# Setting aside rows for DMA engine 4 and raising the cap when levelling the last zero rows of an argmax-scatter kernel

## The chip, the cores and the metric

One core of one Trainium2 chip. The metric is device time in microseconds; lower is better. A run's time is the span of its profile plus about 1.75 us.

## The reference

```python
scores (8, 2048, 2048) float32, values (8, 2048, 2560) float32   # one fixed draw
best_j = argmax(scores, axis=2)
gathered = values[b, best_j]
out = zeros_like(values);  np.add.at(out, (b, best_j), gathered)
```

Row j of a batch of the output is values[b, j] times the number of score rows that chose j. In this draw 6131 output rows are zero (746 in the last batch), 5875 are copied once, and 4378 are scaled by a count of two or more. A row is 10,240 bytes.

## The kernel before: the parts that matter

The kernel moves everything by DMA: score tiles into a ring in SBUF; single rows straight from values to output; scaled rows by a gather, a multiply on ScalarE and a scatter; zero rows by scattering a tile of zeros. An indirect transfer has 128 slots, and slots whose index is out of bounds move nothing. Each of the 16 DMA engines serves eight of the 128 slots of a transfer, so where an index stands decides which engine does the row.

For the last batch's zeros the kernel chooses that. It adds up each engine's rows, adds FETCH (rows set aside for instruction fetches and other things that cost the engine time), and hands the last zero rows to the engines with the least work, at most CORR rows of correction for one engine:

```python
    ZLAST = 12
    FETCH = {2: 5, 3: 12}
    CORR = 56
    # [...]
    for e, n in FETCH.items():
        nc.vector.memset(fetch[:, e:e + 1], float(n))
    # [...] in level_engines: work = zero rows + 2 x scaled rows + fetch + copied rows, per engine
    top = max(work);  more = top - work                # condensed
    more = min(more, CORR) * (zeros <= 16 * (128 - CORR))
    even = ceil(max(zeros - sum(more), 0) / 16)
    quota = more + even                                # running sum; the last engine gets what is left
```

The lines after the second [...] are condensed; in the program each is one VectorE instruction on a 128x16 tile. The last engine (15) takes whatever remains after the running sum, so it gets less than its quota.

At the end GpSimd issues, for the last batch, five gathers, plain copies and zero transfers in turn, five scatters, and the last eight zero transfers with the last three plain copies between them; then it waits until all completions have been counted. Nothing is computed after the last transfer.

## Time and profile before

| | kernel before |
|---|---|
| median of the first 3 runs | 822.98 us (822.6 to 824.76) |
| DMA traffic | 347 MB, 16 engines over 90% busy in 39 of 40 slices |
| the profiled execution, taken apart from these runs | 825.77 us (span 824.0 us) |
| VectorE, the busiest compute engine | 73% |
| last transfer issued | 809.08 us after the start |
| last packet, last completion, end of the span | 821.6, 822.7, 824.0 us |

The lines are in the prediction. The view by windows is to be read as follows: the DMA share is the mean over 16 engines, so 0.0625 in a window of 1 us is one engine busy throughout; the sum of the shares after the first engine runs dry, laid end to end, is where perfectly level engines would stop.

### The profile page before, as it was taken

Reading aid. Unit: us, or ns where it says so; the run is one execution under the profiler, and the core shown is the slowest. Engines: PE = TensorE matmul, PEld = TensorE weight load, DVE = VectorE, ACT = ScalarE, POOL = GpSimd, SP = SyncE. Lnnn points to the kernel's source line nnn. Section 1 sums busy time; section 2 is a strip of 40 time slices with the busy share of each in tenths; the row PEclk is TensorE's granted clock in tenths of the full one; section 3 lists DMA queues with packets and bytes.
Section 4 is the critical chain, followed back from the end, with each engine's and each line's share of the span. In section 5 each row is a group of like instructions: output and inputs, shape, how many; then the busy total and the mean of one; then the engine's idle time right before and its main releaser. Section 6 shows DMA issues by size and latency. Waiting matters only on the chain.

```text
span 824.0 us, 2978 instructions
## 1 busy us (share of the span) xinstructions
PE 31.8 (4%) x786; PEld 29.1 (4%) x786; DVE 600.3 (73%) x737; ACT 168.1 (20%) x107; POOL 271.3 (33%) x277
## 2 busy tenths in 40 slices
PE   0211210000000000000000000000000000000000
PEld 0111110000000000000000000000000000000000
DVE  5887779999999999999999999999998000000000
ACT  6664730041012100023000032000320230230140
POOL 0027241011233504201513200615166356346442
DMA  9999999999999999999999999999999999999997
GB/s 385 426 437 429 433 412 410 441 419 425 427 423 427 428 427 435 429 428 420 429 427 421 429 428 430 433 428 412 426 425 424 423 427 422 424 424 422 425 425 288
DMA packets 44949, 347.12 MB, mean 421 GB/s; under 512 B 18662, under 2 KB 18662, under 8 KB 18662
## 3 DMA queue, kind: packets, MB, share of 16 engines
q0 software_dynamic: 38736, 212.67, 62.1%
q1 hardware_dynamic: 6192, 134.22, 38.0%
q8 instruction: 6, 0.10, 0.0%
q14 instruction: 15, 0.12, 0.0%
HBM read 354.42 MB, written 300.15 MB: 794 GB/s over the span
## 4 chain that ended last, share of the span: by engine, by line
DMA 35%; DVE 27%; another core or an unknown queue 23%; ACT 5%; POOL 5%; issue 4%; PE 0%; SPq 0%; ACTq 0%; POOLq 0%; DVEq 0%
DMA room<-in_values_dram,many_i 23%; DVE am L201 9%; DVE mx L200 9%; DMA out_dram<-room,many_i 8%; DVE mx L224 5%; ACT room L417 4%; DMA room<-in_scores_dram 4%; POOL out_dram L33 3%; ACT less L227 2%; POOL out_dram L182 2%; POOL room L177 1%; DVE oh L378 1%; DVE oh_lo L210 1%; DVE sole L234 0%
## 5 line engine op out<-in xcount | busy, mean ns | idle before, releaser
L201 DVE FIND_INDEX8 am<-mx,room 128x8 uint32<-128x2048 f32 x96 | 219.3, 2285 | 0.0
L200 DVE MAX8 mx<-room 128x8 f32<-128x2048 f32 x96 | 218.7, 2278 | 0.0
L417 ACT ACTIVATE room<-room,many_c 128x2560 f32<-128x2560 f32 x40 | 96.6, 2426 | 587.6 <-DMA room<-in_values_dram,many_i 587.6
L33 POOL DMA_INDIRECT out_dram<-in_values_dram,ones_i x128 | 130.3, 1018 | 106.3 <-DVE m L349 67.9
L182 POOL DMA_INDIRECT out_dram<-room,many_i x40 | 38.7, 966 | 258.0 <-ACT room L417 254.9
L177 POOL DMA_INDIRECT room<-in_values_dram,many_i x40 | 41.2, 1029 | 155.2 <-DMA out_dram<-room,many_i 137.0
L224 DVE MAX8 mx<-room 128x8 f32<-128x2048 f32 x32 | 72.8, 2286 | 11.4 <-DMA room<-in_scores_dram 11.4
L227 ACT ACTIVATE less<-room,mx 128x2048 bf16<-128x2048 f32 x32 | 64.0, 2001 | 38.4 <-DVE sole L234 17.4
L182 POOL DMA_INDIRECT out_dram<-zrow,zero_i x61 | 60.1, 985 | 18.6 <-issue 18.3
L218 PE MATMUL cnt_ps<-oh_hi,oh_lo 128*128 128x16 bf16 x96 | 6.1, 174 | 418.0 <-DVE oh_hi L214 418.0
L218 PEld LDWEIGHTS <-oh_lo 128*128 128x128 bf16 x96 | 6.3, 104 | 417.9 <-DVE oh_lo L210 397.9
L237 PEld LDWEIGHTS <-less 128*128 128x128 bf16 x512 | 16.1, 104 | 83.3 <-ACT less L227 59.6
L378 DVE TENSOR_TENSOR oh<-lo,fill_f 128x2048 f16<-128x2048 uint32 x8 | 18.3, 2291 | 0.3
L237 PE MATMUL cnt_ps<-sole,less 128*128 128x1 bf16 x512 | 18.1, 165 | 0.0
L210 DVE TENSOR_TENSOR oh_lo<-lo,lane_f 128x512 bf16<-128x512 uint32 x24 | 16.6, 693 | 0.4
L234 DVE TENSOR_SCALAR sole<-n_less 128x1 bf16<-128x1 f32 x32 | 4.8, 149 | 14.9 <-ACT less L227 14.7
L201 DVE MATCH_VALUE_LOAD am<-mx,room 128x8 f32 x96 | 8.8, 92 | 3.3
L235 PE MATMUL cnt_ps<-sole,minus 128*128 128x16 bf16 x32 | 5.5, 172 | 82.9 <-DVE sole L234 81.1
L396 PE MATMUL l_ps<-put,oh 128*128 128x32 f16 x128 | 4.7, 188 | 70.9 <-DVE put L393 70.9
L396 PEld LDWEIGHTS <-oh 128*128 128x128 f16 x128 | 4.6, 104 | 72.0 <-DVE oh L378 61.6
L227 ACT ACTIVATION_READ_ACCUMULATOR less<-room,mx 128x1 f32 x32 | 6.0, 186 | 0.0
L206 DVE TENSOR_SCALAR lo<-am 128x4 uint32<-128x4 uint32 x24 | 5.3, 222 | 0.8
(104 smaller groups left out, 80.7 us busy)
## 6 DMA issues: line engine op xcount, KB each, us to landing
room<-in_scores_dram SPq DMA_DIRECT2D x24, 4096.0 KB, 17.5
room<-in_scores_dram SPq DMA_DIRECT2D x9, 2048.0 KB, 13.1
room<-in_scores_dram SPq DMA_DIRECT2D x8, 1024.0 KB, 5.8
room<-in_scores_dram SPq DMA_DIRECT2D x2, 3072.0 KB, 13.9
out_dram<-in_values_dram,ones_i POOLq DMA_INDIRECT x128
out_dram<-zrow,zero_i POOLq DMA_INDIRECT x61
room<-in_values_dram,many_i POOLq DMA_INDIRECT x40, 45.0
out_dram<-room,many_i POOLq DMA_INDIRECT x40, 46.5
```

The source lines that it names most:

```text
L33: return eng.add_instruction(ins)
L177: note(nc.gpsimd.indirect_dma_start(out=v, out_offset=None, in_=values_flat[:, :], in_offset=bass.IndirectOffsetOnAxis(ap=idx, axis=0), bo ...
L182: note(nc.gpsimd.indirect_dma_start(out=out_flat[:, :], out_offset=bass.IndirectOffsetOnAxis(ap=idx, axis=0), in_=v, in_offset=None, bound ...
L200: nc.vector.max(out=mx[:], in_=rows)
L201: nc.vector.max_index(out=am[:, g, :], in_max=mx[:], in_values=rows)
L210: nc.vector.tensor_tensor(out=oh_lo[:], in0=lo[:].unsqueeze(2).to_broadcast([P, G, P]), in1=lane_f[:].unsqueeze(1).to_broadcast([P, G, P]) ...
L218: nc.tensor.matmul(out=cnt_ps[:], lhsT=oh_lo[:, k, :], rhs=oh_hi[:, k, :], start=(t == G - 1 and k == 0), stop=(t == NT - 1 and k == G - 1))
L224: nc.vector.max(out=mx[:], in_=rows)
L227: nc.scalar.activation(out=less[:], in_=rows, func=mybir.ActivationFunctionType.Sign, bias=mx[:, 0:1], scale=-1.0, accum_out=n_less[:])
L237: nc.tensor.matmul(out=cnt_ps[:, c:c + 1], lhsT=less[:, c * P:(c + 1) * P], rhs=w, start=False, stop=(t == NT - 1 and c == NT - 1))
L378: nc.vector.tensor_tensor(out=oh[:], in0=lo[:].unsqueeze(2).to_broadcast([P, NT, P]), in1=fill_f[:].unsqueeze(1).to_broadcast([P, NT, P]), ...
L417: nc.scalar.activation(out=v, in_=v, func=mybir.ActivationFunctionType.Copy, bias=0.0, scale=mc[:, k:k + 1])
```

## The change

Its intent: engine 4 was seen to end late, so 8 rows are set aside for it as well; engine 2 gets one fewer; and the cap that kept engines 9 and 12 from being filled is raised.

```diff
-    FETCH = {2: 5, 3: 12}
-    CORR = 56
+    FETCH = {2: 4, 3: 12, 4: 8}
+    CORR = 64
```

## The prediction

> **What bounds the kernel now.** I read the page first: its head, the table of slices and the queues.
>
> ```profile
> span 824.0 us, 2978 instructions
> PE 31.8 (4%) x786; PEld 29.1 (4%) x786; DVE 600.3 (73%) x737; ACT 168.1 (20%) x107; POOL 271.3 (33%) x277
> DMA  9999999999999999999999999999999999999997
> GB/s 385 426 437 429 433 412 410 441 419 425 427 423 427 428 427 435 429 428 420 429 427 421 429 428 430 433 428 412 426 425 424 423 427 422 424 424 422 425 425 288
> q0 software_dynamic: 38736, 212.67, 62.1%
> q1 hardware_dynamic: 6192, 134.22, 38.0%
> q8 instruction: 6, 0.10, 0.0%
> q14 instruction: 15, 0.12, 0.0%
> ```
>
> No compute engine is over 73% busy, while the 16 DMA engines are over 90% busy in 39 of 40 slices; queues 0 and 1 together hold 100% of their time. The kernel is bound by how long the DMA engines take over 20,762 rows of values and 134 MB of scores. Only the last slice is not full. The view by windows of the end, one window per microsecond (columns: width, five engines' busy time, granted clock, DMA share, GB/s), and the timeline's last line show what is left:
>
> ```profile
> 814.00:815.00 1.00, 0.00 (x0) 0.00 (x0) 0.00 (x0) 0.00 (x0) 0.00 (x0) 1.00 1.01 390
> 815.00:816.00 1.00, 0.00 (x0) 0.00 (x0) 0.00 (x0) 0.00 (x0) 0.00 (x0) 1.00 0.87 349
> 816.00:817.00 1.00, 0.00 (x0) 0.00 (x0) 0.00 (x0) 0.00 (x0) 0.00 (x0) 1.00 0.89 339
> 817.00:818.00 1.00, 0.00 (x0) 0.00 (x0) 0.00 (x0) 0.00 (x0) 0.00 (x0) 1.00 0.63 216
> 818.00:819.00 1.00, 0.00 (x0) 0.00 (x0) 0.00 (x0) 0.00 (x0) 0.00 (x0) 1.00 0.31 73
> 819.00:820.00 1.00, 0.00 (x0) 0.00 (x0) 0.00 (x0) 0.00 (x0) 0.00 (x0) 1.00 0.11 31
> 820.00:821.00 1.00, 0.00 (x0) 0.00 (x0) 0.00 (x0) 0.00 (x0) 0.00 (x0) 1.00 0.08 31
> 821.00:822.00 1.00, 0.00 (x0) 0.00 (x0) 0.00 (x0) 0.00 (x0) 0.00 (x0) 1.00 0.03 0
> 809.08 0.96 POOL L182 DMA_INDIRECT out_dram<-zrow,zero_i  x1 [0.30 <-issue]
> ```
>
> GpSimd issued its last transfer at 809.08, so what comes after is queued work draining, and the engines run dry at different times. The shares from 814 on add up to 1.01+0.87+0.89+0.63+0.31+0.11+0.08+0.03 = 3.93 us of all engines: perfectly level they would end at 817.9. The last packet ended at 821.6, so **3.7 us, 0.45%, is all that any levelling can win**. From 819 to 821, 31 GB/s is about one engine (425/16 = 27): one straggler.
>
> **Which engine.** The packet records of the trace carry time, queue and size but no engine. I chained them: on one engine a packet starts 4 ns before the last one ends, a row of 10,240 B takes 385 ns and a row skipped by the bounds check a 9 ns packet, so a row costs 381 ns and a skipped one 6. Which of an engine's eight rows of each transfer are real follows from the reference's own draw (6131 rows of zeros, 746 in the last batch; 5875 copied once; 4378 scaled), which gives every engine its own pattern; 15 of the 16 chains match one engine's pattern back over most of the run, the other (engine 9) back to 740 us. Ends of the chains, in us: engine 4 821.6; 10 819.8; 3 818.9; 11 818.9; 6 818.6; 14 818.6; 2 818.3; 5 818.1; 1 818.0; 8, 9 and 13 817.4; 7 and 0 816.6; 12 814.7; 15 814.5. The straggler is engine 4, by 1.8 us.
>
> **What the Trainium skill says.** "DMA: Bandwidth & Descriptors", section "The descriptor swizzle", gives partition to engine as 8*(p>>6)+((p>>2)&7); the index layout of this kernel is built on it, and the zero rows match the chains only so: the trace agrees. "Queues, rings and completion order" calls row 14 runtime-internal, one ring per engine; here the 15 packets of queue 14 fall in chains of engine 3 (about 8) and engine 2 (about 6), which is what FETCH answers to. "Latency and other measured facts" says engines 7 and 15 are usually slower; this trace disagrees: 15 ended first, 7 among the first four. "Anatomy of one DMA" says that a completion waits for the write's receipt: here the last data packet ended at 821.35 and the last six completions on the counter that the kernel waits for came at 821.78 to 822.73, 189 ns apart, so a tail of 0.43 us for one mark and 0.19 for each further one.
>
> **The change part by part.** Nothing is added to the stream but one more fill of a 128x1 column: the same row fills 59 ns at 1.1 us, and VectorE waits for its first scores until 5.5, so it costs nothing. The instructions of all other engines are the same. What changes is data: the quota of the last batch's 746 zero rows. I redid the kernel's arithmetic on the reference's draw. Load ahead of the last zeros, engines 0 to 15, before: 1275 1278 1269 1291 1264 1243 1244 1253 1240 1222 1269 1235 1217 1253 1236 1244; after, engine 2 has 1268 and engine 4 has 1272. The top (engine 3, 1291) stays. Corrections of engines 9 and 12 would be 69 and 74; the cap cut both to 56 and now cuts to 64. The even share stays 10. Real zero rows that move: engine 4 37 to 29 (-8), engine 2 32 to 33, engine 9 66 to 74 (+8), engine 12 66 to 74 (+8), engine 15, which takes what is left, 51 to 42 (-9). All others keep theirs.
>
> A moved row is worth 381-6 = 375 ns. If every engine otherwise runs as in this trace, the chains end at: engine 4 821.6-3.0 = 818.6; engine 9 817.4+3.0 = 820.4; engine 12 814.7+3.0 = 817.7; engine 15 814.5-3.4 = 811.1; engine 2 818.7; engine 10 stays at 819.8. The end goes from engine 4 at 821.6 to engine 9 at 820.4, -1.2 us. The tail of completions adds to it: engine 4's last row lay in the last plain copy with six marks behind it (1.38 us); engine 9's 73rd and 74th row lie in the tenth zero transfer, with three marks (0.43+2x0.19 = 0.81). Engine 9's last mark comes at 817.21+3.00+0.81 = 821.0, engine 10's at 819.54+1.38 = 820.9, against 822.73 now. So **the trace taken at its word gives -1.7 us**: 822.98-1.7 = 821.3.
>
> **Rivals.** (a) *The lateness of engine 4 is chance.* Its 1301 rows took 500.3 us, engine 0's 1301 took 496.7. The 3.6 us are stretched packets: three rows at 411 to 413 us (+0.34, +0.39, +0.37), score packets at 421 to 425 (+0.52 in all) and 556 (+0.55), one row at 547 (+0.25), and one instruction fetch at 805 (0.32, and +0.30 on the row beside it). Engine 10 shows stretched packets at 424, 547 and 556 too, and engine 12 two doubled rows at 248 to 249. Unlike engines 2 and 3, engine 4 has only that one fetch of its own. If such stretches fall elsewhere in each run, the end is the latest of some 13 equally loaded engines with a spread of about 1.3 us (from the ends above), and taking one of them out changes the expected end by some 0.1 us. For it: the three times before spread by 2.2 us, as a random straggler would make them. Against it: FETCH values look fitted to observed ends, and a fit of 8 rows for engine 4 matches 3.0 us. Time then: 822.9.
> (b) *A filled-up engine becomes the bound.* Engine 9 gets 8 rows, 3.0 us, though it ended only 4.2 us ahead of engine 4; with a late packet or two it ends where engine 4 did. Time then 822.5 to 823.5. For it: its 820.4 above is the latest end already.
> (c) *Compute or issue takes over.* Against it: GpSimd issues the tenth zero transfer at 806.5, over 10 us before it is due, and the quota arithmetic is over by 634 us. I give it nothing.
>
> **Range and chances.** I weigh the straight reading (821.3) with about 0.45, chance (822.9) with 0.4, a new straggler (823) with 0.15: 822.3. The spread of a median of runs whose own spread was 2.2 us is perhaps 0.8 (an estimate from the three times), so 821.0 to 823.7. A gain of 2% would be 16 us, more than four times what lies open, and nothing added costs even 3 us: within 2% has 0.99.
>
> **What would show it right or wrong.** In the profile after: 128 copies, 61 zero, 40 gather and 40 scatter issues as before, the same 347 MB, DMA share full to about 814; the chains of engine 4 shorter by 8 rows, of 9 and 12 longer by 8, of 15 shorter by 9 and first to end, near 811. If engine 4 ends near 818.6 and engine 9 or 10 last near 820, the straight reading holds; if engine 4 ends near 815 and another engine with stretched packets is last, chance holds; if engine 9 is last after 821, (b). The prediction would be wrong if the chains' ends shifted for all engines, that is if rows took other than 385 ns, or if the row counts above came out differently.

## The result, and the profile after

| | before | changed |
|---|---|---|
| median of 6 runs | 823.62 us (822.6 to 824.76) | 824.69 us (822.69 to 825.44) |
| ratio | | 1.0008, 95% interval 0.9993 to 1.0023 |
| span of the profiled run | 824.0 us | 823.0 us |

A ratio is the mean time of one kernel's runs over the mean of the other's runs of the same rounds, so it is not quite the ratio of the medians. The predicted gain of 0.7 us is not there, and 824.69 lies above the range that ended at 823.7.

What was moved did move. From the page of the changed kernel:

```profile
span 823.0 us, 2979 instructions
GB/s 382 427 439 428 430 422 423 430 430 425 428 432 427 429 420 430 427 428 435 429 421 430 419 434 416 434 418 416 424 426 423 425 425 424 426 420 424 425 424 300
q0 software_dynamic: 38736, 212.67, 62.1%
q1 hardware_dynamic: 6192, 134.22, 38.1%
```

One instruction more (2979 against 2978), the same packets and bytes. The instruction is the fill of engine 4's column; the view of that source line shows three fills of 59 ns at 1.1 us, none of them waited for:

```profile
L117 DVE MEMSET fetch<- x3: 59/59/59, 1.1 to 1.1; 128x1 f32 x3
```

The end of the changed kernel, by windows of 1 us (same columns as in the prediction):

```profile
814.00:815.00 1.00, 0.00 (x0) 0.00 (x0) 0.00 (x0) 0.00 (x0) 0.00 (x0) 1.00 0.91 359
815.00:816.00 1.00, 0.00 (x0) 0.00 (x0) 0.00 (x0) 0.00 (x0) 0.00 (x0) 1.00 1.05 430
816.00:817.00 1.00, 0.00 (x0) 0.00 (x0) 0.00 (x0) 0.00 (x0) 0.00 (x0) 1.00 0.83 298
817.00:818.00 1.00, 0.00 (x0) 0.00 (x0) 0.00 (x0) 0.00 (x0) 0.00 (x0) 1.00 0.51 145
818.00:819.00 1.00, 0.00 (x0) 0.00 (x0) 0.00 (x0) 0.00 (x0) 0.00 (x0) 1.00 0.16 41
819.00:820.00 1.00, 0.00 (x0) 0.00 (x0) 0.00 (x0) 0.00 (x0) 0.00 (x0) 1.00 0.16 62
820.00:821.00 1.00, 0.00 (x0) 0.00 (x0) 0.00 (x0) 0.00 (x0) 0.00 (x0) 1.00 0.04 0
```

From 818 to 820 the share is 0.16, about 2.5 engines, then nothing after 820.6: the one straggler of before has become two that end 1 us earlier. The packet chains, built as in the prediction, name them: engine 7 ends at 820.6 and engine 9 at 820.3. Engine 4 ends at 816.8 (predicted 818.6), engine 12 at 817.6 (817.7), engine 15 first, at 810.6 (811.1). Engine 9 lands where the arithmetic put it (820.4). **Engine 7, which the change does not touch, ended at 816.6 in the first profile and at 820.6 in this one.** That is what the experiments had to explain.

### The profile page after: what moved, and what is told of

Same layout as the page of the kernel before. It is cut to its first block, busy times and chain, and to the rows that moved or that the text cites. A ratio compares the mean times of both kernels' runs of the same rounds, so it can differ in the third digit from the quotient of the medians.

```text
span 823.0 us, 2979 instructions
## 1 busy us (share of the span) xinstructions
PE 31.8 (4%) x786; PEld 29.1 (4%) x786; DVE 599.6 (73%) x738; ACT 168.1 (20%) x107; POOL 273.6 (33%) x277
## 4 chain that ended last, share of the span: by engine, by line
DVE 68%; DMA 25%; ACT 3%; issue 2%; POOL 1%; PE 0%; SPq 0%; ACTq 0%; POOLq 0%; DVEq 0%
DVE am L201 28%; DVE mx L200 26%; DMA room<-in_values_dram,many_i 13%; DMA out_dram<-room,many_i 8%; DVE mx L224 5%; DMA room<-in_scores_dram 4%; ACT less L227 2%; DVE oh L378 2%; DVE oh_lo L210 2%; POOL out_dram L182 1%; ACT room L417 1%; DVE lo L206 1%; DVE oh_hi L214 0%; DVE rank L368 0%; DVE put L393 0%
## 5 line engine op out<-in xcount | busy, mean ns | idle before, releaser
L200 DVE MAX8 mx<-room 128x8 f32<-128x2048 f32 x96 | 218.8, 2279 | 0.0
L214 DVE TENSOR_TENSOR oh_hi<-hi,lane_f 128x64 bf16<-128x64 uint32 x24 | 5.2, 219 | 0.0
```

The lines of the kernel that those rows point to most:

```text
L200: nc.vector.max(out=mx[:], in_=rows)
```

## The experiments

All results in one table first. "Begin" is when VectorE begins the third batch (the first start in the view of the line L200); the chains' ends are worked out from the packet records (a chain is the row of packets that one DMA engine moves one after the other); "last mark" is the last completion on the counter that the kernel waits for. The span ends 1.23 us after the last mark in every profile. Times are medians; each set of rows from one chip shares its runs of the kernel before.

| run | chip | zero rows of engines 4 / 7 / 9 | begin | ends: 4 | 7 | 9 | last chain | last mark | time, us | ratio to before (95%) |
|---|---|---|---|---|---|---|---|---|---|---|
| before, first profile | not listed | 37 / 48 / 66 | 119.7 | 821.6 | 816.6 | 817.4 | 4 | 822.73 | 823.62 | |
| changed, first profile | not listed | 29 / 48 / 74 | 109.0 | 816.8 | 820.6 | 820.3 | 7 | 821.72 | 824.69 | 1.0008 (0.9993 to 1.0023) |
| c1_before_again | 1 | 37 / 48 / 66 | 109.0 | 820.3 | 821.2 | 816.6 | 7 | 822.34 | 825.30 | 0.9999 (0.9985 to 1.0012) |
| e1_fetch_alone | 1 | 30 / 49 / 67 | 109.1 | 815.9 | 819.6 | 817.2 | 11 | 820.89 | 823.64 | 0.9986 (0.9972 to 0.9999) |
| e2_cap_alone | 1 | 36 / 47 / 73 | 109.0 | 819.6 | 821.4 | 819.3 | 7 | 822.50 | 823.99 | 0.9990 (0.9977 to 1.0004) |
| e3_nine_relieved | 1 | 29 / 48 / 71 | 109.0 | 817.2 | 820.2 | 817.6 | 7 | 821.37 | 824.40 | 0.9992 (0.9979 to 1.0006) |
| c2_change_again | 14 | 29 / 48 / 74 | 109.0 | 817.3 | 821.3 | 820.6 | 7 | 822.42 | 825.09 | 1.0002 (0.9989 to 1.0014) |
| g1_seven_relieved | 14 | 29 / 40 / 71 | 109.0 | 816.8 | 818.1 | 817.5 | 11 | 819.57 | 823.10 | 0.9981 (0.9968 to 0.9994) |
| g2_seven_more | 14 | 28 / 55 / 70 | 109.1 | 816.5 | 823.3 | 817.9 | 7 | 824.42 | 827.78 | 1.0028 (1.0015 to 1.0042) |
| t1_by_ends | 14 | 32 / 42 / 69 | 109.0 | 816.7 | 816.2 | 817.4 | 13 | 819.28 | 822.66 | 0.9981 (0.9968 to 0.9994) |
| h1_change_and_seven | 2 | 29 / 40 / 74 | 120.0 | 817.6 | 814.4 | 819.5 | 9 | 820.09 | 823.64 | 0.9986 (0.9973 to 1.0000) |
| h2_before_and_seven | 2 | 38 / 41 / 67 | 120.1 | 821.4 | 814.4 | 817.3 | 4 | 822.56 | 825.09 | 1.0001 (0.9987 to 1.0014) |
| k1_seven_more_again | 2 | 28 / 55 / 70 | 120.0 | 817.5 | 820.9 | 819.1 | 7 | 822.02 | 825.06 (one) | |
| k2_seven_more_again | 2 | 28 / 55 / 70 | 119.9 | 817.8 | 820.4 | 819.3 | 7 | 821.54 | 824.58 (one) | |
| c3_change_third | 4 | 29 / 48 / 74 | 109.4 | 817.9 | 821.6 | 819.9 | 7 | 822.68 | 824.44 | 0.9983 (0.9970 to 0.9997) |
| c4_before_third | 4 | 37 / 48 / 66 | 109.0 | 820.2 | 818.3 | 816.3 | 4 | 821.31 | 825.07 | 0.9999 (0.9985 to 1.0013) |
| g3_relieved_again | 4 | 29 / 40 / 71 | 109.1 | 817.1 | 817.7 | 817.7 | 10 | 819.41 | 822.75 | 0.9971 (0.9958 to 0.9985) |
| t2_both_courses | 4 | 29 / 41 / 68 | 109.0 | 817.7 | 816.6 | 816.6 | 15 | 819.35 | 823.29 | 0.9975 (0.9961 to 0.9989) |

A profile is one execution of the five or so whose median stands in its row; only the first profile of the kernel before (825.77 us) was taken beside the six of its row. The kernel before itself had medians of 823.62, 824.74, 824.63, 824.86 and 825.15 us in the rounds that the changed kernel's first result and these calls shared, so the level moves by 1.5 us from chip to chip or hour to hour. Only the ratios can be compared across calls.

### The two parts alone, and the null

Two theories stood: S, engine 4 is late in every run; C, each run has a straggler by chance. The null is the kernel before under another name; the parts are these edits of it, and the third takes the full change and relieves engine 9:

```diff
 # e1_fetch_alone
-    FETCH = {2: 5, 3: 12}
+    FETCH = {2: 4, 3: 12, 4: 8}
 # e2_cap_alone
-    CORR = 56
+    CORR = 64
 # e3_nine_relieved, against the changed kernel
-    FETCH = {2: 4, 3: 12, 4: 8}
+    FETCH = {2: 4, 3: 12, 4: 8, 9: 8}
```

Expected of c1_before_again: 

> The kernel before, unchanged, under another name: the null of the method. Both theories: ratio to the kernel before 1.000 within 0.002; it shows how far two sets of runs of one program differ by luck. Theory S (engine 4 is late in every run, engine 9 takes its place after the change): in its profile the chain of engine 4 ends last or second to last, 2 us or more after the median of the other chains, near 820.5 us. Theory C (each run has another straggler): engine 4 ends within 1.3 us of the median chain, and some other engine is last.

Expected of e1_fetch_alone: 

> Only the rows set aside (engine 4: 8, engine 2: 4), cap left at 56. By the quota arithmetic engine 4 gets 30 instead of 37 zero rows, engine 9 67 instead of 66, all others one more. Theory S: engine 4 ends near 818 (821 less 7 x 0.375), engine 9 near 817.8, the last chain near 820, so 1 to 1.5 us (0.12 to 0.18%) below the kernel before, and faster than the full change. Theory C: within 0.5 us (0.06%) of the kernel before.

Expected of e2_cap_alone: 

> Only the cap, 64 instead of 56. Engine 9 gets 73 instead of 66 zero rows, engine 12 73 instead of 66, all others one fewer. Theory S: engine 4 still last near 820 to 821, engine 9 second near 820.0; the time as before within 0.5 us. Theory C: as before within 0.5 us too, with any engine last; the ends of the chains tell the two apart, not the time.

Expected of e3_nine_relieved: 

> The full change, and 8 rows set aside for engine 9 as well: its zero rows fall from 74 to 71, engine 15 takes the 3. Theory S: engine 9 ends 1.1 us earlier than the 820.3 of the changed kernel, near 819.2, so the last chain ends near 819.5 unless another is stretched: 0.5 to 1 us below the changed kernel. Theory C: no difference from the changed kernel beyond 0.5 us.

The null gave 0.9999, so the method is sound to some 0.0013. The rows set aside alone gained 0.14%, as S said, with engine 11 last. But neither theory named the last engine. In the profiles of the null and of e2 engine 4 is late as S said (820.3 and 819.6), and yet engine 7 is last in both, at 821.2 and 821.4, which S had not named. Against C, the last is not a new engine each time: it is engine 7 in the changed kernel's first profile, in c1, e2 and e3. The cap alone and e3 lie within the noise of the kernel before. That led to theory D: engine 7 is usually the last, and the change does not touch it.

### Relieving and loading engine 7

Against e3, only engine 7's entry differs; the fourth kernel levels all engines on the mean ends seen so far:

```diff
 # g1_seven_relieved
-    FETCH = {2: 4, 3: 12, 4: 8, 9: 8}
+    FETCH = {2: 4, 3: 12, 4: 8, 7: 8, 9: 8}
 # g2_seven_more
-    FETCH = {2: 4, 3: 12, 4: 8, 9: 8}
+    FETCH = {2: 4, 3: 12, 4: 8, 7: -8, 9: 8}
 # t1_by_ends, against the kernel before
-    FETCH = {2: 5, 3: 12}
-    CORR = 56
+    FETCH = {1: 3, 2: 7, 3: 16, 4: 8, 5: 4, 6: 3, 7: 9, 8: 5, 9: 13, 10: 6, 11: 5, 12: 12, 13: 1, 14: 2, 15: 8}
+    CORR = 80
```

Expected of c2_change_again: 

> The changed kernel, unchanged, on the same chip as the three that follow. Theory D (formed on the six profiles so far: engine 7 ends near 820.6 us in the profiles of the changed kernel, of the kernel before run again, of the cap alone and of engine 9 relieved, and the change does not touch it): engine 7 or 9 ends last, near 820.5; ratio to the kernel before 1.000 within 0.001. Theory C (chance alone): another engine is last; same ratio.

Expected of g1_seven_relieved: 

> The kernel of e3 (full change and 8 rows for engine 9) with 8 rows set aside for engine 7 too: its zero rows go from 48 to 40, engine 15 takes them. Theory D: engine 7 ends at 820.6 less 3.0 = 817.6, the last chain is then engine 8, 10 or 11 near 819; about 1.5 us (0.18%) below the kernel before. Theory C: no difference beyond 0.5 us from the kernel before, as another engine is last by chance.

Expected of g2_seven_more: 

> The kernel of e3 with engine 7 loaded instead: 55 zero rows in place of 48, all others one fewer or so. Seven rows of 375 ns are 2.6 us. Theory D: engine 7 ends near 823.2 and is last in every run; about 2 us (0.25%) above the kernel before, and little spread between runs. Theory C: if engine 7 is usual (near 817.8) it now ends at 820.4, and the time rises by 1 us at most.

Expected of t1_by_ends: 

> All 16 engines levelled on the mean ends of the chains in the six profiles so far (between 0 and 16 rows set aside for every engine, cap 80): zero rows 29 23 33 9 32 57 57 42 59 69 29 64 75 50 66 52. Theory D: means level near 817.5, so with the spread of 0.6 to 1.6 us per engine the last ends near 819: 1.5 to 2 us (0.2%) below the kernel before, faster than both kernels. Theory C: the last ends near 820 to 821 whatever the quotas; within 0.5 us of the kernel before.

These decide it. The end of g2 by windows:

```profile
819.00:820.00 1.00, 0.00 (x0) 0.00 (x0) 0.00 (x0) 0.00 (x0) 0.00 (x0) 1.00 0.10 31
820.00:821.00 1.00, 0.00 (x0) 0.00 (x0) 0.00 (x0) 0.00 (x0) 0.00 (x0) 1.00 0.07 31
821.00:822.00 1.00, 0.00 (x0) 0.00 (x0) 0.00 (x0) 0.00 (x0) 0.00 (x0) 1.00 0.06 20
822.00:823.00 1.00, 0.00 (x0) 0.00 (x0) 0.00 (x0) 0.00 (x0) 0.00 (x0) 1.00 0.05 20
823.00:824.00 1.00, 0.00 (x0) 0.00 (x0) 0.00 (x0) 0.00 (x0) 0.00 (x0) 1.00 0.03 0
```

From 820 to 823 a share of 0.05 to 0.07 is one engine of 16 at work: engine 7, which ends at 823.3 where 823.2 was forecast from seven rows of 375 ns. The end of g1:

```profile
816.00:817.00 1.00, 0.00 (x0) 0.00 (x0) 0.00 (x0) 0.00 (x0) 0.00 (x0) 1.00 0.86 308
817.00:818.00 1.00, 0.00 (x0) 0.00 (x0) 0.00 (x0) 0.00 (x0) 0.00 (x0) 1.00 0.51 134
818.00:819.00 1.00, 0.00 (x0) 0.00 (x0) 0.00 (x0) 0.00 (x0) 0.00 (x0) 1.00 0.10 11
819.00:820.00 1.00, 0.00 (x0) 0.00 (x0) 0.00 (x0) 0.00 (x0) 0.00 (x0) 1.00 0.00 0
```

With engine 7 relieved the share falls from 0.51 to nothing within 2 us and no single engine is left over. The time follows: 0.9981 with engine 7 relieved, 1.0028 with it loaded, 1.0002 for the change alone, on the same chip. One expectation failed: g2 was to have little spread, and its six times fell into two groups, 825.05 and 825.43 against 827.51 to 828.12. t1 did no better than g1, which gives other quotas than the kernel before to six engines only. D leaves one result open: e1 leaves engine 7 with 49 rows, one more than before, and still gained 0.14%; in its one profile engine 7 ended at 819.6. It was not run again.

### Two courses of the same program

The views of the line L200 in the first profile of the kernel before, and in that of the changed kernel:

```profile
L200 DVE MAX8 mx<-room x96: 2273/2276/2290, 119.7 to 617.1; 128x8 f32<-128x2048 f32 x96
```

```profile
L200 DVE MAX8 mx<-room x96: 2274/2276/2291, 109.0 to 605.4; 128x8 f32<-128x2048 f32 x96
```

The third batch begins 10.7 us later in the first. All profiles up to then but that first one began at 109. The timeline of ScalarE shows where it comes from, before and then changed:

```profile
72.21 0.19 ACT L227 ACTIVATION_READ_ACCUMULATOR less<-room,mx 128x1 f32 x1
77.69 2.00 ACT L227 ACTIVATE less<-room,mx 128x2048 bf16<-128x2048 f32 x1 [5.30 <-remote]
79.60 0.19 ACT L227 ACTIVATION_READ_ACCUMULATOR less<-room,mx 128x1 f32 x1
85.52 2.00 ACT L227 ACTIVATE less<-room,mx 128x2048 bf16<-128x2048 f32 x1 [5.73 <-issue]
```

```profile
72.31 0.18 ACT L227 ACTIVATION_READ_ACCUMULATOR less<-room,mx 128x1 f32 x1
72.81 2.00 ACT L227 ACTIVATE less<-room,mx 128x2048 bf16<-128x2048 f32 x1 [0.31 <-DVE sole L234]
74.72 0.19 ACT L227 ACTIVATION_READ_ACCUMULATOR less<-room,mx 128x1 f32 x1
75.01 2.00 ACT L227 ACTIVATE less<-room,mx 128x2048 bf16<-128x2048 f32 x1
```

ScalarE twice stands still for over 5 us, for a reason that the profile names only as "remote" and "issue". Neither stop is in the other course. The DMA engines stay full (shares of 0.99 and 1.00 from 60 to 100 us), so the time is not lost; but all that follows runs beside other transfers. The traces differ in one more thing. In the five profiles of the 120 us course (this one and four below) 95 to 116 of the 4992 completion records of the DMA are missing, the first from transfers that landed at 71 to 74 us, where ScalarE stops; in the 13 others none is missing. Whether the recording of the profile takes part in the stops was not tested. To see whether the groups of g2 are these courses, it was looked at twice more, unchanged. Two other kernels asked whether engine 7 or engine 9 alone explains the gain:

```diff
 # h1_change_and_seven, against the changed kernel
-    FETCH = {2: 4, 3: 12, 4: 8}
+    FETCH = {2: 4, 3: 12, 4: 8, 7: 8}
 # h2_before_and_seven, against the kernel before
-    FETCH = {2: 5, 3: 12}
+    FETCH = {2: 5, 3: 12, 7: 8}
```

Expected of h1_change_and_seven: 

> The changed kernel with 8 rows set aside for engine 7 as well, engine 9 left full (74 zero rows). Theory D, with engine 9 as the new straggler: engine 7 ends near 818, engine 9 last near 820.4, so only 0.3 to 1 us below the changed kernel, and about 1 us above the kernel in which engine 9 was relieved too. Rival: engine 9 is harmless and the last is near 819; then 1.5 us below the kernel before, as with both relieved.

Expected of h2_before_and_seven: 

> The kernel before with 8 rows set aside for engine 7 alone (zero rows 41 in place of 48; engine 4 gets 38 in place of 37). Theory D: engine 7 ends near 818, engine 4 is last near 820.3: 0.5 to 1 us below the kernel before. Rival (engine 4 does not matter at all): the last is near 819, 1.5 us below.

Expected of k1_seven_more_again: 

> The kernel with seven more rows on engine 7 once more, one look: its six times lay in two groups, 825.05 and 825.43 against 827.51 to 828.12. Theory: the groups are two courses of the run. In the usual one VectorE begins the third batch at 109 us and engine 7 ends near 823; in the other, which the first profile of the kernel before shows (119.7 us), engine 7 escapes some 3 us of stretched packets and ends near 820. Rival: one course, and the groups are chance.

Expected of k2_seven_more_again: 

> The same look again, as one of three runs fell in the faster group: theory and rival as for the look before it; a time near 825.3 must go with a begin near 119.7 us and an engine 7 that is not last, a time near 828 with 109 us and engine 7 last.

Both took 825.06 and 824.58 us, began at 120.0 and 119.9, and engine 7 ended at 820.9 and 820.4 against 823.3: this fits the two groups being the two courses, as far as three profiles can show it. (The chip is a rival: all four profiles are from chip 2, and no other profile has the 120 us course except the first, whose chip is not listed. Against it, both groups of g2 came from chip 14.) The expectation that engine 7 would not be last there failed; with seven more rows it still is, by 1 to 2 us.

All four profiles were of the 120 us course; which course the other runs took is not known. h1 and h2 differ by exactly the change, and in both engine 7 is out of the way (814.4). Engine 4 is last without the change (821.4) and 817.6 with it, engine 9 then being last at 819.5. The ratios 0.9986 and 1.0001 differ by 0.15%, 1.2 us; the medians differ by 1.45 us, and the slowest run of h1 (824.22) lies below the fastest of h2 (824.25). **With engine 7 relieved in both, the change gains the 1.2 us or so that was predicted.** The rival that engine 4 does not matter at all (h2 1.5 us below the kernel before) fell: h2 gained nothing, not even the 0.5 to 1 us that theory D gave it.

Taking all 18 profiles, and putting every chain back to the zero rows of the kernel before at 375 ns per row:

| course | profiles | engine 4 ends (mean, standard deviation) | engine 7 ends |
|---|---|---|---|
| third batch begun at 109 us | 13 | 820.0, 0.7 | 820.3, 1.2 |
| third batch begun at 120 us | 5 | 821.1, 0.4 | 817.4, 0.6 |

So engine 4 is late in both courses, and engine 7 as late as engine 4 in one. The packet records of the same program in both courses, the first profile and c1, show where engine 7 loses its time: between 200 and 600 us its packets were stretched beyond their usual duration by 0.2 us in all in the first, and by more than 4 us in c1; its ends differ by 4.6 us. In the 109 us course such stretches come back at the same moments in nearly every profile, for instance at 420 to 421 us a row of engines 4, 7, 8 or 9 takes 371 to 421 ns more than its 385. What stretches them stays open.

### A last check, and a kernel for both courses

```diff
 # t2_both_courses, against the kernel before
-    FETCH = {2: 5, 3: 12}
-    CORR = 56
+    FETCH = {1: 3, 2: 8, 3: 17, 4: 11, 5: 4, 6: 5, 7: 10, 8: 4, 9: 14, 10: 6, 11: 5, 12: 13, 13: 1, 14: 3, 15: -2}
+    CORR = 80
```

Expected of c3_change_third: 

> The changed kernel a third time. If its profile is of the 109 us course: engine 7 last near 820.5 to 821, time as before within 1 us. If of the 120 us course: engine 4 ends near 818, engine 7 near 817.4, engine 9 last near 820, and the time about 1 to 1.5 us below the kernel before in the same course.

Expected of c4_before_third: 

> The kernel before a third time, the null. 109 us course: engine 7 last near 820.5, engine 4 near 819.4. 120 us course: engine 4 last near 821, engine 7 near 817.4. In both the last chain is near 821, so no difference in time between the courses for this kernel.

Expected of g3_relieved_again: 

> Engines 4, 7 and 9 all relieved, again: in either course the last chain is engine 10 or 11 near 818.5 to 819.2; 1.2 to 2 us (0.15 to 0.25%) below the kernel before.

Expected of t2_both_courses: 

> Levelled for the later of the two courses' mean ends per engine: zero rows 29 23 32 8 29 57 55 41 60 68 29 64 74 50 65 62. The last chain is expected near 818.5 to 819 in either course, 1.5 to 2.5 us (0.2 to 0.3%) below the kernel before; a rival says that the spread of single engines (0.3 to 1.1 us) keeps it where the kernel with engines 4, 7 and 9 relieved is.

All four profiles fell in the 109 us course, so the changed kernel itself was never profiled in the other. Engine 7 was last in c3 again (821.6). In c4 it was not (818.3): even within the course it is late in 9 of 13 profiles (820.2 or later, put back to the same rows), not in all. The changed kernel measured 0.9983 here, after 1.0008 and 1.0002: the three average to 0.9998, and why they differ is not shown. The kernel that relieves engines 4, 7 and 9 gave 0.9981 and 0.9971, t1 0.9981 and t2 0.9975: all four results are below the kernel before, with intervals that exclude 1. By the medians of the same call they beat the kernel before and the changed kernel by 1.2 to 2.4 us, but are fitted to this one draw. The rival that t2 gains nothing over g3 stands.

## Why the prediction was wrong, point by point

- **What bounds the kernel** was right: the end of the slowest DMA engine. Seven rows more on engine 7 moved its end by what 375 ns per row says, and the span ended 1.23 us after the last mark in every profile.
- **The arithmetic of the quotas and of a moved row** was right: engine 9 ended at 820.3 for 820.4, engine 12 at 817.6 for 817.7, engine 15 at 810.6 for 811.1. Engine 4 came 1.8 us earlier than forecast: with the rows of the kernel before, its end of 816.8 is one of 819.8, as is usual in the 109 us course. Two sums slip: the weights give 822.2 and not 822.3, and the stretched packets listed for engine 4 add up to 3.0 of the 3.6 us.
- **The step that failed** is the one put as "if every engine otherwise runs as in this trace". The term that it mis-sized is engine 7's end: taken as 816.6, and 820.6 in the profile after; 820.3 on average in the commoner course. The single profile read was of the rarer course, and of a long execution: it took 825.77 us, and the gain read in it was taken off a median of 822.98, that is off runs that already ended 2.8 us earlier. With engine 7 at 820.6 the last packet goes from 821.6 to 820.6, not to 820.4 with the shorter tail of engine 9; and in the same course the last packet comes no earlier with the change (820.6, 821.3 and 821.6 in the first profile, c2 and c3) than without it (821.2 and 820.2 in c1 and c4).
- **The straight reading** (-1.7 us) came out, nearly, only where engine 7 was out of the way: h1 against h2 shows 1.2 to 1.45 us. It was given a weight of 0.45 for all runs.
- **Rival (a), chance,** was wrong about engine 4, which is late in both courses (820.0 and 821.1 at the same rows), and about the stretches, which return at the same moments. Its forecast of 0.1 us came closer than the straight reading for another reason: a second engine is as late in the commoner course.
- **Rival (b), engine 9,** is half right. It is last in h1 and second last in the first and second profile of the changed kernel. The time gained by relieving it alone (e3) is not clear of noise.
- **Rival (c)** was rightly given nothing: the last zero transfer was issued at 809.1 us before and at 808.9 us after.
- **The range** was also set from three runs with a median of 822.98. Six runs gave 823.62, so 0.6 us of the miss of 2.4 us is the baseline and 0.7 us the missing gain; the rest is the 1.1 us by which the medians differ, which is within the noise (1.0008 by the means, interval 0.9993 to 1.0023).

## What to carry to other kernels

When 16 queues drain in parallel and the slowest sets the end, relieving one of them is worth the distance to the next one, and that distance has to come from several profiles: one profile can show a rare course of the program in which another queue is first. A cheap test of who sets the end is to load a suspect by a known amount: if the time rises by that amount, it was the bound (here 2.7 us between c2 and g2, for seven rows worth 2.6). Before tuning by tenths of a per cent, run the unchanged kernel under a second name, and look for groups among the times.

## What the Trainium skill lacked or had wrong

- "DMA: Bandwidth & Descriptors", section "Latency and other measured facts", names engines 7 and 15 as usually slower. Here it depends on the run: engine 7, put back to the same rows, ended at 820.3 us on average in 13 profiles (late) and at 817.4 in 5 (early), engine 15 always among the first (about 814.5). Engine 4 is late in both groups (820.0 and 821.1).
- The same page has nothing on packets that take about twice their usual time at recurring moments of a program: rows of 385 ns took 756 to 806 ns at 420 to 421 us in the profiles of the commoner course.
- No page that I read says that one program can take two courses, 11 us apart at the third batch (109 and 120 us) with the same total DMA work. What stops ScalarE for 5.3 and 5.7 us there, no run here shows.
- The section "Queues, rings and completion order" calls row 14 runtime-internal without saying which engines carry it or what it costs. Here its packets of 8 KB (309 ns each) fall on engines 3 (seven or eight) and 2 (about six) and a few others; on engine 3 the row beside one often takes 0.35 us longer as well.
- "Anatomy of one DMA" gives the receipt of the last write as the main part of the fixed cost. Here the completions of one engine also follow each other at 0.19 to 0.21 us, so six of them behind the last row add 1 us to the end.
